# An attention and gMLP block on one core: weight differences behind the softmax scaling, and rotation tables by one transpose

## The chip, the cores and the metric

The kernel runs on one core of a Trainium2 chip. The metric is the device time in microseconds. A core has a matrix engine (TensorE, PE in the profile), VectorE (DVE), ScalarE (ACT), GpSimd (POOL) and SyncE (SP), which here only issues transfers. ACT and POOL issue transfers too, in the same queue of instructions as their other work. Each engine takes its own queue in order, and an instruction waits for semaphores that other engines and transfers raise.

## The reference

One block over 1024 positions of width 1024, all in float32: an RMS norm, one input projection, windowed attention with sinks, a gated branch with position mixing, two merge gates, an output projection, the residual and a last RMS norm. What matters here is the attention's part:

```python
q = partial_rope(q.reshape(B, S, ATT_HEADS, HEAD_DIM), pos)
k = partial_rope(k.reshape(B, S, ATT_KV_HEADS, HEAD_DIM), pos)
...
m = jnp.maximum(jnp.max(s, axis=-1, keepdims=True), sink)
p = jnp.exp(s - m)
denom = jnp.sum(p, axis=-1, keepdims=True) + jnp.exp(sink - m)
o = jnp.einsum('bhgnqk,bnkhd->bnqhgd', p / denom, vb.astype(jnp.float32))
```

There are 16 query heads of 64 and 2 heads of keys and values; the window goes by chunks of 64 positions. `partial_rope` turns the first 16 of the 64 values of a head by the cosine and sine of a position times 8 frequencies, so the tables hold 8 x 1024 numbers each.

## The kernel before, in words

**Products.** Every projection goes by a scheme of seven products in place of eight (Strassen's). `gemm_pair` makes one pair of row blocks: seven times `product`, 12 matmuls each of 128x512, in the order b11, t1, t2, b21, t3, b22, t4. Each operand is split in two float32r parts, a high one (`wh`) and a low one (`wl`), and a product is made of high times high, high times low and low times high. The weights of the next pair are split while the present one runs: four times per pair `split_next` takes the next halves (`wr` loaded, or `s`, the sums that the scheme needs) and calls `split`: ACT casts the high part (L176) and DVE subtracts it, which leaves the low part (L177, the *weight difference*). With 1024 columns it serves two products.

**Stages in order.** First norms and the gMLP's parts; then one pair for keys and values; then four pairs for q (m = 0, 2, 4, 6), during which keys and q are rotated; then eleven pairs for the gates z, gs and ga, into whose hooks the attention's steps are woven; then the gated branches, the merge and the output projection.

**The attention's steps.** There are 32. For each chunk `softmax_stage` has two score matmuls (L1445), copies on ACT (L1451), one bound per half on DVE (L1457: sum of two halves and their row minimum), and the exponential on ACT (L1473). At the step's end it takes the sink's exponential (L1487, L1488), adds it to the sums (L1489), takes the reciprocal (L1491) and scales the weights `pr` with it (L1497). `weight_stage` turns the scaled weights by PE transposes (L1518); `value_stage` multiplies them with the values (L1553, L1558).

**Order.** The code of pairs and steps is interleaved by hooks between the products. A scheduler then orders each engine's queue by its own estimates of when things are ready, and `after(a, b)` adds an order between two instructions of one engine without a wait.

**Tables.** In the q stage the rotation (by DVE, on rows that are turned so that positions lie along the row) needs the tables as 128x512 tiles: row (half, head, frequency), column position. `rope_tables`, a generator that runs in the hooks of the second q pair (m = 2), loads cos and sin with positions on the partitions, spreads them on DVE (L1221, eight copies), turns them on PE (L1228, eight transposes in two groups of four) and copies each table out on ACT (L1229). The steps of `steps_of_q` run one after the other: tables first, then the keys' rotations, then q's.

**Transfers.** The stores of q and the loads of weights go through SP's queue, the stores of keys and values through POOL's, and ACT's queue has no transfer but a load at the start (L109). Eight semaphores go round among the transfers that SP and ACT issue: each waits until the one that used its semaphore before is done.

Of the kernel before, what the change touches and what calls it, by code (L numbers as in the profile page):

```python
# [24 lines left out]
F32 = mybir.dt.float32  # L25
# [5 lines left out]
P = 128  # L31
D = 1024
S = 1024
KC = D // P
HALF = 512
NT = S // P
# [16 lines left out]
def hybrid_tile(  # L53
# [16 lines left out]
    nc = tc.nc  # L70
# [42 lines left out]
    ident = const.tile([P, P], F32, name="ident")  # L113
# [21 lines left out]
    k_dr = scratch("k_dr", (P, 4, S))  # L135
    v_dr = scratch("v_dr", (NT, P, 2, 3 * HD))
    s1_dr = scratch("s1_dr")
    z_dr = scratch("z_dr")
    gs_dr = scratch("gs_dr")
    ga_dr = scratch("ga_dr")  # L140
# [26 lines left out]
    hi_of, lo_of = [], []  # L167
# [51 lines left out]

    of_units = []  # L220
    bounds = []
    sums_behind = []

    def split_next():

        if not units:
            begin_job()
        if not units:
            return
        halves, keys = units.pop(0)  # L230
        if keys[0][1] == 2:
            make_sums(term_of_x11[0] if done[0] <= 4 else None)
        hi = mtile([P, D], F32R, "wh", 3)
        lo = mtile([P, D], F32R, "wl", 3)
        if isinstance(halves, list):
            for c, half in enumerate(halves):
                split(hi[:, half_of(c)], lo[:, half_of(c)], half)
        else:
            wide = halves.shape[1]
            first = split(hi[:, 0:wide], lo[:, 0:wide], halves)  # L240
            if keys[0] == (done[0] - 1, 6) and done[0] > LAST_OF_Q + 2:
                if bounds:
                    sums_behind.append(first)
                else:
                    make_sums(first)
        of_units.append(hi_of[-1])
        for c, key in enumerate(keys):
            ready[key] = hi[:, half_of(c)], lo[:, half_of(c)]
        if len(units) == 1:
            begin_job()  # L250

    def half_of(half):
        return slice(half * HALF, (half + 1) * HALF)
# [19 lines left out]
    def make_sums(first=None):  # L273

        while sums_to_make:
            sums_to_make.pop(0)(first)
# [269 lines left out]
    pool = outer.enter_context(tc.tile_pool(name="mixing", bufs=1))  # L546
# [527 lines left out]
    late = []  # L1074
# [82 lines left out]
    pool = stage.enter_context(tc.tile_pool(name="keys", bufs=1))  # L1157
# [32 lines left out]
    def finish(i, half, q, src, sign):  # L1190
        if sign < 0:
            nc.scalar.mul(q[:], src, sign)
        (values_of if i else keys_of)(half, q)

    gemm_pair(hb, finish, hook)
    stage.close()

# [4 lines left out]
    pool = stage.enter_context(tc.tile_pool(name="queries", bufs=1))  # L1202
    split_pool = stage.enter_context(tc.tile_pool(name="split", bufs=1))
    SC = -(HD**-0.5)
    tables = []

    def rot_tile():
        return mtile([P, HALF], F32, "rot", 5, pool)

    both = rot_tile()[:, 0 : 2 * NT * 16].rearrange("p (f t d) -> p f t d", f=2, t=NT)  # L1210

    def rope_tables():

        for f, src in enumerate((cos, sin)):
            nc.sync.dma_start(both[:, f], src)
        yield
        for src in (both[:, 0, :, 0:8], both[:, 1, :, 8:16]):
            tab = mtile([P, HALF], F32, f"tab{len(tables)}", 1, pool)
            wide = rot_tile()
            for i in range(4):  # L1220
                nc.vector.tensor_copy(  # L1221
                    wide[:, i * P : (i + 1) * P].rearrange("p (a h d) -> p a h d", a=2, h=8),
                    src[:, i : i + 5 : 4, :].unsqueeze(2).broadcast_to([P, 2, 8, 8]),
                )
            yield
            pt = bank("tp")
            for i in range(4):
                nc.tensor.transpose(pt[:, i * P : (i + 1) * P], wide[:, i * P : (i + 1) * P], ident[:])  # L1228
            nc.scalar.copy(tab[:], pt[:])  # L1229
            tables.append(tab)  # L1230
            yield

# [103 lines left out]
    for m in range(0, KC, 2):  # L1336

        def finish(i, half, q, src, sign):
            if sign < 0:
                nc.scalar.mul(q[:], src, sign)  # L1340
            put(q_raw, m + i, half, q[:])
            rows = slice((m + i) * P, (m + i + 1) * P)
            split_q(q[:], [(slice(0, P), q_hl[:, rows, half_of(half)].rearrange("a p t -> p a t"))])

        if m == 2:
            steps_of_q.append(rope_tables())
        if m == 4:
            steps_of_q.append(rotate_keys(0))
            steps_of_q.append(rotate(0, 3))
        gemm_pair(hb, finish, part_of_q)  # L1350
# [76 lines left out]
    def softmax_stage(g, t, par, qt):  # L1427

        kt = keys[g, t][0]
        q_of = qt[:].rearrange("p i (q c) -> p c (i q)", c=2)
        nmax, sums = small(), small()
        n_pr[0] += 1
        pr = mtile([P, 2, 384], F32, f"pr{n_pr[0] % 2}", 1, weights_pool)
        held_in = {}
        sinks_of = (v[:, 4 * g + par : 4 * g + par + 3 : 2] for v in (sink_sb, nsink_sb))
        sk, nsk = sinks_of
        for c in range(2):
            lo, hi = window_of(t, c)  # L1440
            wide = hi - lo
            scores, halves, copies = [], [], []
            for i in range(2):
                sc = bank("sc")[:, 0 : 2 * wide].rearrange("p (f k) -> p f k", f=2)
                nc.tensor.matmul(  # L1445
                    sc, q_of[:, c, i * P : (i + 1) * P], kt[:, :, lo:hi], start=True, stop=True
                )
                scores.append(sc)
            for i, sc in enumerate(scores):
                two = mtile([P, 2, 192], F32, "sl", 2, aheads)[:, :, 0:wide]  # L1450
                copies.append(nc.scalar.copy(two, sc))  # L1451
                halves.append(two)
            for i, two in enumerate(halves):
                at = 192 * (1 - c) if t else P * (1 - c)
                held_in[c, i] = v = pr[:, i, at : at + wide]
                bounds.append(
                    nc.vector.tensor_tensor_reduce(  # L1457
                        v,
                        two[:, 0, :],
                        two[:, 1, :],  # L1460
                        1.0,
                        nsk[:, i : i + 1],
                        op0=ALU.add,
                        op1=ALU.min,
                        accum_out=nmax[:, 1 - c, i : i + 1],
                    )
                )
# [12 lines left out]

            unfinished.append(rest_of_chunk)
            if c == 0:
                yield

        def rest_of_step():
            es = small()
            nc.vector.tensor_add(es[:], sk.unsqueeze(1).broadcast_to([P, 2, 2]), nmax[:])  # L1487
            nc.scalar.activation(es[:], es[:], AF.Exp)  # L1488
            nc.vector.tensor_add(es[:], es[:], sums[:])  # L1489
            inv = small()  # L1490
            nc.vector.reciprocal(inv[:], es[:])  # L1491
            spans = ((0, 2, 384),) if t else ((0, 1, P), (1, 1, 64))
            start = 0
            for first, chunks, wide in spans:
                v = pr[:, :, start : start + wide].rearrange("p i (c k) -> p i c k", c=chunks)
                by = inv[:, first : first + chunks].rearrange("p c i -> p i c").unsqueeze(3)
                nc.vector.tensor_mul(v, v, by.broadcast_to(list(v.shape)))  # L1497
                start += wide
            held.append(pr)

        yield
# [531 lines left out]
    for p in range(4):  # L2033
# [93 lines left out]
        wide = HALF // 2  # L2127
# [98 lines left out]
```

## Time and profile before

| what | us |
|---|---|
| median of 3 runs | 890.01 (889.78 to 890.14) |
| the profiled execution, its time | 890.97 |
| the profiled execution, its span | 889.2 |
| DVE COPY of the tables (L1221), x8 | 0.22 each |
| ACT COPY of the tables (L1229), x2 | 0.59 each |
| PE transposes of the tables (L1228), from 232.1 to 238.4 | 8 |
| attention's transposes (L1518), from 315.8 to 573.2 | 184 |

The page gives busy times of each engine over the span. A row of a timeline has the start, the duration, the engine, the line, the operation, and out<-in by the program's names; behind it in brackets stands how long the engine had been idle and what released it. A row of the chain of waits has the start, the length, the engine, what it made and the line: it is the work that ended last, followed back from the end, step by step to what released it. A matmul's duration overlaps that of the next, so what a matmul costs is read from the distance of two starts.

### The profile page before, as it was taken

What the parts mean: (1) busy time and instruction counts of PE and PEld (TensorE: products, weight loads), DVE (VectorE), ACT (ScalarE), POOL (GpSimd) and SP (SyncE); (2) the same over time, 40 slices, a digit from 0 to 9 for tenths busy, and PEclk for the clock granted to TensorE, in tenths of its full rate; (3) what the DMA queues carried; (4) which work ended last, traced back from release to release, by engine and by line L of the source; (5) the groups of instructions that cost most, each with busy time, mean ns of one, the idle gap of its engine ahead of it and who ended that gap; (6) DMA issues with size and microseconds to landing.
All of it is one profiled execution on the core that took longest, in us unless ns stands there. A gap on an engine that the chain in (4) does not pass through costs nothing.

```text
span 889.2 us, 13055 instructions
## 1 busy us (share of the span) xinstructions
PE 879.4 (99%) x4117; PEld 731.3 (82%) x4117; DVE 696.5 (78%) x1334; ACT 557.0 (63%) x1125; POOL 150.9 (17%) x217
## 2 busy tenths in 40 slices
PE   9999999999999999999999999999999999999996
PEld 6888888888888888888888888888888888888885
DVE  7869966566687679989888999847796587579886
ACT  6865533334455478888878888864684485467443
POOL 3322222203030001111211111101121121110012
PEclk9999999999999999999999999999999999999999
DMA  9998888958778666887786789989899789998533
GB/s 331 217 266 220 269 206 177 172 153 259 257 256 282 215 198 182 217 187 191 179 242 227 227 234 232 240 303 375 310 294 373 270 233 253 299 308 285 177 120 118
DMA packets 131409, 212.39 MB, mean 239 GB/s; under 512 B 12778, under 2 KB 59882, under 8 KB 131340
## 3 DMA queue, kind: packets, MB, share of 16 engines
q1 hardware_dynamic: 108808, 148.62, 49.9%
q0 software_dynamic: 22384, 62.67, 31.6%
q8 instruction: 33, 0.54, 0.2%
q14 instruction: 36, 0.29, 0.1%
q10 hardware_dynamic: 148, 0.27, 0.1%
HBM read 146.37 MB, written 86.11 MB: 261 GB/s over the span
## 4 chain that ended last, share of the span: by engine, by line
PE 93%; DMA 2%; DVE 2%; ACT 2%; issue 1%; SPq 0%; ACTq 0%
PE ps_mm L362 44%; PE ps_o L362 23%; PE ps_tp L362 7%; PE ps_sc L362 3%; PE ps_tp L796 2%; PE ps_sc L1445 2%; PE ps_tp L1518 2%; PE ps_o L796 2%; PE ps_mm L796 2%; PE ps_tp L1115 2%; PE ps_o L1553 1%; PE ps_sc L796 1%; DMA T_t1l<-in_x_dram 1%; DMA T_t3h<-in_w_dram 1%; PE ps_o L1558 1%
## 5 line engine op out<-in xcount | busy, mean ns | idle before, releaser
L176 ACT CAST wh<-s 128x1024 fp32r<-128x1024 f32 (+1 forms) x79 | 79.4, 1007 | 75.2 <-PE ps_mm L362 23.2
L177 DVE TENSOR_TENSOR wl<-wr,wh 128x512 fp32r<-128x512 f32 (+1 forms) x77 | 72.0, 936 | 59.9 <-ACT wh L176 56.5
L176 ACT CAST wh<-wr 128x512 fp32r<-128x512 f32 (+1 forms) x77 | 63.1, 820 | 61.1 <-PE ps_mm L362 38.7
L177 DVE TENSOR_TENSOR wl<-s,wh 128x1024 fp32r<-128x1024 f32 (+1 forms) x79 | 92.8, 1175 | 10.2 <-ACT wh L176 10.1
L1451 ACT COPY sl<-ps_sc 128x384 f32<-128x384 f32 (+2 forms) x128 | 52.0, 458 | 15.5 <-DVE sm L1457 11.5
L362 PE MATMUL ps_o<-T_t1h,wh 128*128 128x512 f32 x148 | 58.0, 392 | 0.0
L362 PE MATMUL ps_o<-T_t1h,wl 128*128 128x512 f32 x148 | 57.8, 390 | 0.0
L362 PE MATMUL ps_o<-T_t1l,wh 128*128 128x512 f32 x148 | 57.6, 389 | 0.0
L1473 ACT ACTIVATE pr<-pr,sm 128x192 f32<-128x192 f32 (+2 forms) x128 | 56.6, 450 | 0.0
L362 PE MATMUL ps_mm<-T_b11h,wh 128*128 128x512 f32 x140 | 54.9, 392 | 0.0
L362 PE MATMUL ps_mm<-T_b11l,wh 128*128 128x512 f32 x140 | 54.6, 390 | 0.0
L362 PE MATMUL ps_mm<-T_t3h,wh 128*128 128x512 f32 x140 | 54.6, 390 | 0.0
L362 PE MATMUL ps_mm<-T_t2l,wh 128*128 128x512 f32 x140 | 54.6, 390 | 0.0
L362 PE MATMUL ps_mm<-T_t2h,wh 128*128 128x512 f32 x140 | 54.6, 390 | 0.0
L362 PE MATMUL ps_mm<-T_t3l,wh 128*128 128x512 f32 x140 | 54.6, 390 | 0.0
L362 PE MATMUL ps_mm<-T_b11h,wl 128*128 128x512 f32 x140 | 54.6, 390 | 0.0
L362 PE MATMUL ps_mm<-T_t3h,wl 128*128 128x512 f32 x140 | 54.6, 390 | 0.0
L362 PE MATMUL ps_mm<-T_t2h,wl 128*128 128x512 f32 x140 | 54.5, 389 | 0.0
L362 PE MATMUL ps_mm<-T_t4h,wh 128*128 128x512 f32 x136 | 53.2, 391 | 0.0
L362 PE MATMUL ps_mm<-T_t4h,wl 128*128 128x512 f32 x136 | 53.0, 390 | 0.0
L362 PE MATMUL ps_mm<-T_t4l,wh 128*128 128x512 f32 x136 | 52.9, 389 | 0.0
L1457 DVE CUSTOM_DVE_ANT_0 pr<-sl,nsink_sb 128x192 f32<-128x192 f32 (+2 forms) x128 | 47.3, 400 | 3.5 <-ACT sl L1451 2.5
(431 smaller groups left out, 2435.3 us busy)
## 6 DMA issues: line engine op xcount, KB each, us to landing
wr<-in_w_dram SPq DMA_DIRECT2D x86, 256.0 KB
sums<-in_w_dram POOLq DMA_DIRECT2D x20, 512.0 KB, 6.8
s<-sums SPq DMA_DIRECT2D x20, 512.0 KB
q_hl<-qhl SPq DMA_DIRECT2D x16, 512.0 KB
q<-q_hl SPq DMA_DIRECT2D x64, 128.0 KB
y_dr<-x POOLq DMA_DIRECT2D x28, 256.0 KB, 6.9
g<-in_w_dram POOLq DMA_DIRECT2D x12, 512.0 KB, 6.8
wr<-in_w_dram SPq DMA_DIRECT2D x11, 512.0 KB
```

Of the source, the lines that this page charges most:

```text
L176: hi_of.append(nc.scalar.copy(hi, src))
L177: lo_of.append(nc.vector.tensor_sub(lo, src, hi.bitcast(F32)))
L362: nc.tensor.matmul(acc, lt, rt, start=fresh and k == 0 and n == 0, stop=k == 3 and n == 2, skip_group_check=True,)
L796: mm = nc.tensor.matmul(acc[:], lt, rt, start=fresh and k == 0 and n == 0, stop=stops and k == 3 and n == terms[-1], skip_group_check=True,)
L1115: nc.tensor.matmul(pm[:, t * P : (t + 1) * P], xh[:, half * 4 + t, g * P : (g + 1) * P], bias[-1][1][:, g % 4, :], start=True, stop=True,)
L1445: nc.tensor.matmul(sc, q_of[:, c, i * P : (i + 1) * P], kt[:, :, lo:hi], start=True, stop=True)
L1451: copies.append(nc.scalar.copy(two, sc))
L1457: nc.vector.tensor_tensor_reduce(v, two[:, 0, :], two[:, 1, :], 1.0, nsk[:, i : i + 1], op0=ALU.add, op1=ALU.min, accum_out=nmax[:, 1 - c, ...
L1473: e = nc.scalar.activation(v, v, AF.Exp, bias=nmax[:, 1 - c, i : i + 1], scale=-1.0, accum_out=sums[:, 1 - c, i : i + 1])
L1518: nc.tensor.transpose(dst, pr[:, i, block * P : block * P + width], ident[:])
L1553: nc.tensor.matmul(po[:, first], va[1][:, vs], a[:, n, first], start=n == 0, stop=n == 1, skip_group_check=True)
L1558: nc.tensor.matmul(po[:, cs], vb[c][:, vs], b[c][:], start=t == 0, stop=True, skip_group_check=True)
```

## The change

It has two parts.

**The differences.** The list `scaled_steps` collects the scalings. Once there are bounds and a scaling, `split_next` puts each weight difference that it issues behind the last scaling that has been issued, on DVE, by `after`.

**The tables.** In the pair for keys and values, cos and sin are loaded on SP (`load_tables`) into a tile of their own, two DVE copies put the 8 used columns of each beside one another (`pack_tables`, 128x64 each), one PE transpose of 128x128 turns both, ACT copies the result (`turn_tables`), and two transfers on ACT's queue store it to a scratch tensor `rope_dr` in DRAM. In the q stage `rope_tables` loads each table from there by two transfers on ACT's queue, which read every row eight times, once for each head. The generator joins `steps_of_q` at the first q pair (m = 0) in place of the second, so what follows it, the rotation of the keys, can begin earlier.

```diff
     def split_next():
...
+        if bounds and scaled_steps:
+            after(lo_of[-1], scaled_steps[-1])
         of_units.append(hi_of[-1])
...
+    def load_tables():
+        for f, src in enumerate((cos, sin)):
+            nc.sync.dma_start(both[:, f], src)
+
+    def pack_tables():
+        for f in range(2):
+            nc.vector.tensor_copy(
+                narrow[:, 64 * f : 64 * f + 64].rearrange("p (n d) -> p n d", n=NT),
+                both[:, f, :, 8 * f : 8 * f + 8],
+            )
+
+    def turn_tables():
+        pt = bank("tp")
+        nc.tensor.transpose(pt[:, 0:P], narrow[:], ident[:])
+        nc.scalar.copy(turned[:], pt[:, 0:P])
+        for f in range(2):
+            nc.scalar.dma_start(rope_dr[f].rearrange("d (n p) -> n d p", n=NT), turned[64 * f : 64 * f + 64])
...
+    late += [load_tables, pause, pause, pause, pack_tables, pause, pause, turn_tables]
     gemm_pair(hb, finish, hook)
...
     def rope_tables():
-        for f, src in enumerate((cos, sin)):
-            nc.sync.dma_start(both[:, f], src)
-        yield
-        for src in (both[:, 0, :, 0:8], both[:, 1, :, 8:16]):
-            tab = mtile([P, HALF], F32, f"tab{len(tables)}", 1, pool)
-            wide = rot_tile()
-            for i in range(4):
-                nc.vector.tensor_copy(
-                    wide[:, i * P : (i + 1) * P].rearrange("p (a h d) -> p a h d", a=2, h=8),
-                    src[:, i : i + 5 : 4, :].unsqueeze(2).broadcast_to([P, 2, 8, 8]),
-                )
-            yield
-            pt = bank("tp")
-            for i in range(4):
-                nc.tensor.transpose(pt[:, i * P : (i + 1) * P], wide[:, i * P : (i + 1) * P], ident[:])
-            nc.scalar.copy(tab[:], pt[:])
+        for f in range(2):
+            tab = mtile([P, HALF], F32, f"tab{f}", 1, pool)
+            for half in range(2):
+                nc.scalar.dma_start(
+                    tab[64 * half : 64 * half + 64],
+                    rope_dr[f][:, half_of(half)].unsqueeze(0).broadcast_to([8, 8, HALF]),
+                )
             tables.append(tab)
             yield
...
-        if m == 2:
+        if m == 0:
             steps_of_q.append(rope_tables())
...
-                nc.vector.tensor_mul(v, v, by.broadcast_to(list(v.shape)))
+                scaled_steps.append(nc.vector.tensor_mul(v, v, by.broadcast_to(list(v.shape))))
```

How this moves instructions. The lines of the changed kernel are higher by 1 up to the list, by 4 up to the tables and by 18 behind them.

DVE before, at the end of a step in the second gate pair (around 348 us of the span); `sm` are sums and bounds, `ISA` is a bound, `pr` the softmax weights:

```order
L1487 TENSOR_TENSOR sm_3287<-sink_sb,sm_3166 128x4
L404 TENSOR_TENSOR x_3045<-x_3045,ps_o_3095 128x512
L1489 TENSOR_TENSOR sm_3287<-sm_3287,sm_3167 128x4
L177 TENSOR_TENSOR wl_3309<-s_3019,wh_3308 128x1024
L1491 RECIPROCAL sm_3291<-sm_3287 128x4
L1457 ISA pr_557_3274,sm_3272<-sl_3316,nsink_sb 128x192
L1457 ISA sm_3272 128x1
L1497 TENSOR_TENSOR pr_531_3168<-pr_531_3168,sm_3291 128x768
L1457 ISA pr_557_3274,sm_3272<-sl_3318,nsink_sb 128x192
L1457 ISA sm_3272 128x1
L177 TENSOR_TENSOR wl_3343<-s_3020,wh_3342 128x1024
```

The same place of DVE after the change:

```order
L1505 TENSOR_TENSOR sm_3279<-sink_sb,sm_3158 128x4
L408 TENSOR_TENSOR x_3037<-x_3037,ps_o_3087 128x512
L1507 TENSOR_TENSOR sm_3279<-sm_3279,sm_3159 128x4
L1475 ISA pr_556_3266,sm_3264<-sl_3308,nsink_sb 128x192
L1475 ISA sm_3264 128x1
L1509 RECIPROCAL sm_3283<-sm_3279 128x4
L1475 ISA pr_556_3266,sm_3264<-sl_3310,nsink_sb 128x192
L1475 ISA sm_3264 128x1
L1515 TENSOR_TENSOR pr_530_3160<-pr_530_3160,sm_3283 128x768
L178 TENSOR_TENSOR wl_3301<-s_3011,wh_3300 128x1024
L178 TENSOR_TENSOR wl_3335<-s_3012,wh_3334 128x1024
```

The first difference has moved from ahead of the reciprocal to behind the scaling, and the second bound has moved ahead of the scaling. It is so in nine pairs; at step 1 the difference moves behind the scaling too, and there PE's four transposes go ahead of two score matmuls that they followed. On ACT the two exponentials that need these bounds go ahead of an eviction (L535) that they followed.

PE before, in the second q pair, where the first of the two groups of table transposes stands between products t2 and b21:

```order
L362 MATMUL ps_mm_2059<-T_t2h_693,wh_2019 128x512
L362 MATMUL ps_mm_2059<-T_t2l_694,wh_2019 128x512
L362 MATMUL ps_mm_2059<-T_t2h_693,wl_2020 128x512
L1228 MATMUL ps_tp_2115<-ident,rot_2093 128x128 x4
L362 MATMUL ps_o_2121<-T_b21h_142,wh_1973 128x512
L362 MATMUL ps_o_2121<-T_b21l_143,wh_1973 128x512
```

PE after, in the pair for keys and values, between products b21 and t3:

```order
L366 MATMUL ps_o_1782<-T_b21h_143,wh_1615 128x512
L366 MATMUL ps_o_1782<-T_b21l_144,wh_1615 128x512
L366 MATMUL ps_o_1782<-T_b21h_143,wl_1616 128x512
L1215 MATMUL ps_tp_1809<-ident,narrow_1728 128x128
L366 MATMUL ps_mm_1730<-T_t3h_755,wh_1688 128x512
L366 MATMUL ps_mm_1730<-T_t3l_756,wh_1688 128x512
```

Both groups of four are gone from the second q pair, and one transpose has come into the pair before the q stage.

ACT before, in the first q pair (from about 213 us on); `qhl` is a q cast, `x` an eviction:

```order
L176 CAST wh_1973<-wr_1872 128x1024
L1240 ACTIVATE qhl_1968<-x_1906 128x4x2x64
L1240 ACTIVATE qhl_1991<-x_1908 128x4x2x64
L176 CAST wh_2019<-s_1882 128x1024
L1240 ACTIVATE qhl_2010<-x_1907 128x4x2x64
L176 CAST wh_2043<-s_1883 128x1024
L1340 ACTIVATE x_2035<-ps_mm_1905 128x512
```

ACT after, at the same place:

```order
L177 CAST wh_1991<-wr_1885 128x1024
L1258 ACTIVATE qhl_1986<-x_1918 128x4x2x64
L1244 DMA tab_298_1934<-rope_dr 64x1x512 x2
L1244 DMA tab_300_1951<-rope_dr 64x1x512 x2
L1258 ACTIVATE qhl_2009<-x_1920 128x4x2x64
L1258 ACTIVATE qhl_2028<-x_1919 128x4x2x64
L177 CAST wh_2037<-s_1895 128x1024
L177 CAST wh_2061<-s_1896 128x1024
L1358 ACTIVATE x_2053<-ps_mm_1917 128x512
```

The four table loads stand behind the first q cast, and one more q cast now stands ahead of the cast of the weights for product t1 of the next pair. POOL's order is unchanged. On SP, the two loads of cos and sin stand among the sums' stores of the pair for keys and values, and the loads for the rotation of the keys come earlier by part of a pair.

More of the change, by code (lines that the diff above doesn't have):

```diff
@@ L137, in hybrid_tile @@
     s1_dr = scratch("s1_dr")
+    rope_dr = scratch("rope_dr", (2, 8, S))
     z_dr = scratch("z_dr")
@@ L221, in hybrid_tile @@
     bounds = []
+    scaled_steps = []
     sums_behind = []
@@ L1193, in finish, with pause @@
         (values_of if i else keys_of)(half, q)
+    both = mtile([P, 2, NT, 16], F32, "both", 1, pool)
+    narrow, turned = (mtile([P, P], F32, tag, 1, pool) for tag in ("narrow", "turned"))
+    def load_tables():
[13 more added lines that the diff above has]
+            nc.scalar.dma_start(rope_dr[f].rearrange("d (n p) -> n d p", n=NT), turned[64 * f : 64 * f + 64])
+    def pause():
+        pass
+    late += [load_tables, pause, pause, pause, pack_tables, pause, pause, turn_tables]
     gemm_pair(hb, finish, hook)
@@ L1208, in rot_tile @@
         return mtile([P, HALF], F32, "rot", 5, pool)
-    both = rot_tile()[:, 0 : 2 * NT * 16].rearrange("p (f t d) -> p f t d", f=2, t=NT)
     def rope_tables():
-        for f, src in enumerate((cos, sin)):
-            nc.sync.dma_start(both[:, f], src)
-        yield
-        for src in (both[:, 0, :, 0:8], both[:, 1, :, 8:16]):
-            tab = mtile([P, HALF], F32, f"tab{len(tables)}", 1, pool)
-            wide = rot_tile()
-            for i in range(4):
-                nc.vector.tensor_copy(
-                    wide[:, i * P : (i + 1) * P].rearrange("p (a h d) -> p a h d", a=2, h=8),
-                    src[:, i : i + 5 : 4, :].unsqueeze(2).broadcast_to([P, 2, 8, 8]),
-                )
-            yield
-            pt = bank("tp")
-            for i in range(4):
-                nc.tensor.transpose(pt[:, i * P : (i + 1) * P], wide[:, i * P : (i + 1) * P], ident[:])
-            nc.scalar.copy(tab[:], pt[:])
+        for f in range(2):
[4 more added lines that the diff above has]
+                    rope_dr[f][:, half_of(half)].unsqueeze(0).broadcast_to([8, 8, HALF]),
+                )
             tables.append(tab)
```

## The prediction

> **What bounds the kernel now.** I read the page's busy table and its chain first, then what PE waits for, then the chain and the timelines at single places.
>
> ```profile
> span 889.2 us, 13055 instructions
> PE 879.4 (99%) x4117; PEld 731.3 (82%) x4117; DVE 696.5 (78%) x1334; ACT 557.0 (63%) x1125; POOL 150.9 (17%) x217
> PE 93%; DMA 2%; DVE 2%; ACT 2%; issue 1%; SPq 0%; ACTq 0%
> PE ps_tp L1518 <- DVE pr L1497: 0.6, 2, 0.4
> ```
>
> PE is busy for 99% of the span and carries 93% of the chain. So only two things are worth time: work taken off PE, and moments in which PE stands still. Work taken off DVE (78%) or ACT (63%) is worth nothing by itself. The fourth line is the only wait of PE inside the attention stage that the waits name: the transposes of the softmax weights (L1518) stood for the scaling on DVE (L1497), twice, 0.6 us in all. Since matmul ends are modelled, I don't trust that sum and go by starts instead: matmuls of one product start 0.22 or 0.23 us apart.
>
> ```profile
> 349.68 0.39 PE L362 MATMUL ps_mm<-T_b11h,wl 128*128 128x512 f32 x1
> 350.46 0.30 PE L1518 MATMUL ps_tp<-ident,pr 128*128 128x128 f32 x1 [0.40 <-DVE pr L1497]
> 375.67 0.39 PE L362 MATMUL ps_mm<-T_b11h,wl 128*128 128x512 f32 x1
> 375.90 0.27 PE L1518 MATMUL ps_tp<-ident,pr 128*128 128x128 f32 x1
> 401.07 0.39 PE L362 MATMUL ps_mm<-T_b11h,wl 128*128 128x512 f32 x1
> 401.53 0.30 PE L1518 MATMUL ps_tp<-ident,pr 128*128 128x128 f32 x1
> 501.48 0.39 PE L362 MATMUL ps_mm<-T_b11h,wl 128*128 128x512 f32 x1
> 501.89 0.30 PE L1518 MATMUL ps_tp<-ident,pr 128*128 128x128 f32 x1
> 552.50 0.39 PE L362 MATMUL ps_mm<-T_b11h,wl 128*128 128x512 f32 x1
> 552.96 0.30 PE L1518 MATMUL ps_tp<-ident,pr 128*128 128x128 f32 x1
> ```
>
> At 375.67 the transposes follow after 0.23, with no stall. At 349.68 they follow after 0.78, at 401.07 after 0.46, at 501.48 after 0.41 and at 552.50 after 0.46. The stalls are 0.55, 0.23, 0.18 and 0.23: **1.19 us**, twice what the waits name. All stand at the same point, between the first product of a pair (b11) and the transposes of a step.
>
> **The change, part 1: the weight difference behind the scaling.** What DVE does just ahead of the largest stall:
>
> ```profile
> 347.74 0.16 DVE L1489 TENSOR_TENSOR sm<-sm,sm 128x4 f32<-128x4 f32 x1
> 347.82 1.22 DVE L177 TENSOR_TENSOR wl<-s,wh 128x1024 fp32r<-128x1024 f32 x1
> 348.96 0.17 DVE L1491 RECIPROCAL sm<-sm 128x4 f32<-128x4 f32 x1
> 349.05 0.39 DVE L1457 CUSTOM_DVE_ANT_0 pr<-sl,nsink_sb 128x192 f32<-128x192 f32 x1
> 349.36 0.95 DVE L1497 TENSOR_TENSOR pr<-pr,sm 128x768 f32<-128x768 f32 x1
> 350.23 0.41 DVE L1457 CUSTOM_DVE_ANT_0 pr<-sl,nsink_sb 128x192 f32<-128x192 f32 x1
> 350.57 1.22 DVE L177 TENSOR_TENSOR wl<-s,wh 128x1024 fp32r<-128x1024 f32 x1
> ```
>
> A difference of 1.22 us stands between the sums and their reciprocal. Starts give the slots: the difference 1.14 (347.82 to 348.96), the reciprocal 0.09, a bound 0.31 to 0.34, the scaling 0.87. The new order has sums, bound, reciprocal, bound, scaling, difference, difference. So the scaling loses 1.14 ahead of it and gains one bound (0.34): it starts at 349.36 - 1.14 + 0.34 = 348.56 and ends at 349.51. PE started 0.15 after the scaling's end (350.31 to 350.46), so it could start at 349.66. The end of the product allows 349.68 + 0.23 = 349.91. The stall is gone with 0.25 us to spare; at the other three places it was smaller by 0.3 or more for the same move, so these go too. I take all of 1.19; the bounds are 0 (something else is late there) and 1.19.
>
> What is late next? The first difference now runs from 349.43 to 350.65 and the second ends where it did. The first one's reader is the third matmul of the pair's second product:
>
> ```profile
> 351.97 0.40 PE L362 MATMUL ps_o<-T_t1h,wl 128*128 128x512 f32 x1
> 325.69 0.61 PE ps_tp L1518 x4
> 350.46 0.85 PE ps_tp L1518 x6
> ```
>
> Without the stall it stands at 351.97 - 0.55 = 351.42, and with 0.15 for the hand-over the difference has to end by 351.27: 0.62 us of slack. At step 1 (325.69) the four transposes only change places with two score matmuls; I take nothing there.
>
> **Part 2: one transpose for eight.**
>
> ```profile
> 229.57 2.72 PE ps_mm L362 x12
> 232.30 0.50 PE ps_tp L1228 x4
> 232.79 2.76 PE ps_o L362 x12
> 238.28 0.44 PE ps_tp L1228 x4
> L1221 DVE COPY rot<-rot x8: 218/219/220, 231.8 to 232.7; 128x128 f32<-128x128 f32 x8
> L1229 ACT COPY tab<-ps_tp x2: 587/590/592, 233.1 to 238.8; 128x512 f32<-128x512 f32 x2
> ```
>
> The eight old transposes stand on PE's chain with 0.50 + 0.44 = 0.94 us, between products with no gap, so all of it goes. The product behind one costs 2.76 for 2.72, which I leave inside the error. One transpose comes instead, between two products of the key and value pair. No row shows a lone one. From the rows above, four cost 0.61 and six 0.85 in the softmax, so 0.12 each and 0.61 - 3 x 0.12 = 0.25 for one; from 0.44 it is 0.44 - 3 x 0.12 = 0.08. I take 0.20, nearer to the row with the same matmuls on both sides of a step; the bounds are 0.08 and 0.25. The net is **0.74 us** (0.69 to 0.86). The Trainium skill, "TensorE: Matmul & The Clock Gate", section "Part 4: PE-mode transpose", gives about 275 ns for one 128x128 transpose inside a kernel (in bf16); by that price, an estimate, the net would be 0.66 and the sum 0.08 less. This trace doesn't show a lone one in fp32.
>
> The 8 copies on DVE (8 x 0.219 = 1.8 us) and the 2 on ACT (1.2 us) are worth nothing, since PE didn't wait for either engine there; nor do the two new copies of 128x64 and one of 128x128 cost anything, as long as they arrive before PE's new transpose some 10 us later.
>
> **Part 3: six DMAs on ACT's queue.** The two stores of the turned table stand where ACT idled before, and two loads more on SP stand ahead of stores of the sums. The four table loads stand in ACT's queue right behind the first q cast of the first q pair:
>
> ```profile
> 216.74 0.67 ACT L1240 ACTIVATE qhl<-x 128x512 fp32r<-128x512 f32 x1
> 219.45 0.66 ACT L1240 ACTIVATE qhl<-x 128x512 fp32r<-128x512 f32 x1 [2.04 <-DVE x L398]
> 221.28 1.05 ACT L176 CAST wh<-s 128x1024 fp32r<-128x1024 f32 x1 [1.17 <-PE ps_o L362]
> 214.44 2.53 SPq L212 DMA_DIRECT2D wr<-in_w_dram  x4
> 217.07 0.54 SPq L523 DMA_DIRECT2D q_raw<-x  x1
> 212.39 0.77 POOL L1183 DMA_DIRECT2D v_dr<-vt  x1 [3.70 <-issue]
> 216.59 0.53 POOL L1258 MEMSET rot<- 128x512 f32 x1 [3.43 <-DMA v_dr<-vt]
> 227.14 0.39 PE L362 MATMUL ps_o<-T_t1h,wl 128*128 128x512 f32 x1
> y_dr<-x POOLq DMA_DIRECT2D x28, 256.0 KB, 6.9
> ```
>
> Their waits are: the last store of the values (landed by 216.59), the stores of the table, and, since eight semaphores go round among the DMAs of SP and ACT, the weight loads of 214.44 and the q store of 217.07. Behind them in ACT's queue stand two q casts (0.66 each) and the cast of the weights for the next pair's second product (1.05), behind which DVE makes the difference (1.22) that PE reads at 227.14. Counted back: 227.14 - 0.15 - 1.22 - 1.05 - 0.66 - 0.66 = 223.4 is when ACT must be free at the latest. Without any wait it is free at 217.41 + 4 x 0.54 = 219.57 (0.54 is the issue of a store above). How long a store of 256 KB takes to land on SP's queue no row shows; the value store of 212.39 needed 4.2 us, which gives 217.07 + 4.2 + 0.54 = 221.8: 1.6 us of slack. I take no cost; the bounds are 0 and 1.1 (if it lands after 6.9 us, the median of POOL's stores y_dr on the page: 217.07 + 6.9 + 0.54 = 224.5).
>
> The Trainium skill, "DMA: Bandwidth & Descriptors", section "Anatomy of one DMA — SWDGE (gpsimd) path", says that DMA engines never wait on semaphores and that the issuing engine's sequencer does it before dispatch. This rule speaks against putting such loads on a computing engine; it is the mechanism of the third case below, and no run so far shows it, as ACT's queue carries one load only (L109) before the change.
>
> POOL's own order doesn't move. On SP the loads for the key rotation come earlier, and PE waits for nothing of theirs.
>
> **Sum.** 1.19 + 0.74 = 1.93 us. The profiled execution took 890.97 (span 889.2 and 1.8 around it), 0.96 above the median of 890.01. 890.97 - 1.93 = 889.04 for a profiled one, and 890.01 - 1.93 = **888.1** for the median. A measurement of this kernel can tell about 0.2% from no change, which is 1.78 us, so the forecast lies just beyond that bound.
>
> **The rivals.**
>
> 1. *The scaling isn't what PE waited for alone.* If ACT's work for the same step, or the second bound in front, keeps the transposes late, only the tables and a part of the stalls remain: 0.74 + 0.3 = 1.0, 889.0. For it speaks that the spare time at 349.9 is only 0.25 us; against it, that the scaling's end and PE's start lie 0.15 apart at every stall.
> 2. *The second bound becomes the late one (slower).* The scaling now stands behind both bounds, and these wait for ACT's copies of the scores. If the copy for the second one comes late by d, the four stalling pairs lose d - 0.25 each, on top of a gain of 1.93. The point is 4 x (d - 0.25) = 1.93, d = 0.73 us; with d = 1.2 the loss is 3.8 - 1.9 = 1.9 us: 891.9. The row below is ACT's two copies of that step: they are done at 346.75 + 0.86 = 347.61, and the second bound now starts at about 348.25, 0.64 later, which speaks against it; for it speaks only that ACT's order moves around there.
>
> ```profile
> 346.75 0.86 ACT L1451 COPY sl<-ps_sc 128x384 f32<-128x384 f32 x2 [2.35 <-DVE sm L1457]
> ```
>
> 3. *ACT stands at the table loads.* At 6.9 us of landing PE loses 224.5 - 223.4 = 1.1 us once, and the result is 889.2; at 8 us it is 890.3. A pair later ACT has caught up, because it is busy for only 63%.
> 4. *More goes than counted*: the 0.04 behind a transpose, the changed places at step 1, another short stall. 887.7.
>
> **How the numbers follow.** The forecast has 0.55, and with 0.3 us either way about four fifths of it lie beyond 0.2%: 0.44 faster, 0.11 same. Rival 1 has 0.17 and rival 3 0.12, both same; rival 2 has 0.10, slower; rival 4 has 0.06, faster. Faster 0.50, same 0.40, slower 0.10. The range goes from 887.5, below rival 4, to 889.8, above rivals 1 and 3 up to a landing of 7.5 us; rival 2 and the tail of 3 are left out.
>
> **What the profile of after would show.** Right: the waits of PE name L1515 (the scaling's new line) once at most, at the last step near 571 us, which isn't reordered; b11's last matmul and the transposes lie 0.23 apart in every pair; no wait of PE for a weight difference; the rows of L1228 are gone from the chain and one transpose stands at about 197 us. Wrong: gaps above 0.23 at those places (rival 1 or 2; the releaser of the second bound tells which), a wait of PE for the weights between 226 and 230 us, or ACT idle there until after 223.4 (rival 3).

## The result, and the profile after

| | median us | range | runs |
|---|---|---|---|
| before | 890.2 | 889.78 to 890.79 | 9 |
| after | 887.84 | 887.17 to 889.1 | 9 |

The ratio is 0.9971, with a 95% interval of 0.9963 to 0.998: faster by 2.4 us of the medians, and by 1.8 to 3.3 us by the interval. The profiled execution of `diffs_only` was disturbed (3160 us) and is left out of its median, so that part's trace is read from `diffs_only_2`.

The page after the change: the busy times, and the chain by engine.

```profile
span 885.7 us, 13043 instructions
PE 877.2 (99%) x4110; PEld 731.4 (83%) x4110; DVE 696.2 (79%) x1328; ACT 555.3 (63%) x1124; POOL 151.6 (17%) x217
PE 97%; ACT 1%; DVE 1%; issue 0%; DMA 0%; ACTq 0%
```

What PE waits for after the change (in all, times, longest), the one line inside the attention stage:

```profile
PE ps_tp L1536 <- DVE pr L1515: 0.2, 1, 0.2
```

DVE and ACT are as busy as before. PE's share of the chain has gone from 93% to 97%, as the chain leaves PE less often. Of the two waits for the scaling one is left, at the last step; it stood there before too (0.17 of the 0.6 us). PE's timeline after the change, at the four places that had a stall:

```profile
348.00 0.39 PE L366 MATMUL ps_mm<-T_b11h,wl 128*128 128x512 f32 x1
348.23 0.81 PE L1536 MATMUL ps_tp<-ident,pr 128*128 128x128 f32 x6
398.80 0.39 PE L366 MATMUL ps_mm<-T_b11h,wl 128*128 128x512 f32 x1
399.03 0.27 PE L1536 MATMUL ps_tp<-ident,pr 128*128 128x128 f32 x1
498.94 0.39 PE L366 MATMUL ps_mm<-T_b11h,wl 128*128 128x512 f32 x1
499.17 0.27 PE L1536 MATMUL ps_tp<-ident,pr 128*128 128x128 f32 x1
549.74 0.39 PE L366 MATMUL ps_mm<-T_b11h,wl 128*128 128x512 f32 x1
549.97 0.27 PE L1536 MATMUL ps_tp<-ident,pr 128*128 128x128 f32 x1
```

Each distance is 0.23 us; they were 0.78, 0.46, 0.41 and 0.46. All 1.19 us are gone, and a little more goes with them, because the matmuls behind a stall run a little slower. From b11's last matmul to the third matmul of the next product, with the transposes and two scores between, it was 351.97 - 349.68 = 2.29 us at the first place and is 349.70 - 348.00 = 1.70: 0.59 less, where the distance alone says 0.55. At the other three the same stretch is shorter by 0.27, 0.23 and 0.28. That is 1.37 us in all.

Six transposes in the chain of waits, before the change at a place without a stall (the prediction shows 0.85 for the six at 350.46, behind a stall):

```profile
376.06 0.65 PE ps_tp L1518 x6
```

And after the change at the first of the four places:

```profile
348.39 0.65 PE ps_tp L1536 x6
```

The chain counts a row behind a stall from its own start, and other rows from the end of the matmul before, so 0.85 and 0.65 don't compare as prices. By starts the six cost 0.60 behind the stall (350.46 to 351.06, where the scores start) and 0.57 after the change (348.23 to 348.80).

The timeline of DVE at the first of these places, and in the last line PE's reader of the first difference:

```profile
346.03 0.16 DVE L1507 TENSOR_TENSOR sm<-sm,sm 128x4 f32<-128x4 f32 x1
346.11 0.41 DVE L1475 CUSTOM_DVE_ANT_0 pr<-sl,nsink_sb 128x192 f32<-128x192 f32 x1
346.86 0.95 DVE L1515 TENSOR_TENSOR pr<-pr,sm 128x768 f32<-128x768 f32 x1
347.73 2.35 DVE L178 TENSOR_TENSOR wl<-s,wh 128x1024 fp32r<-128x1024 f32 x2
349.70 0.40 PE L366 MATMUL ps_o<-T_t1h,wl 128*128 128x512 f32 x1
```

The scaling begins 0.83 us behind the start of the sums (it was 1.62), and ends at 347.81, 0.42 before PE takes it. The first of the two differences ends at about 348.9, 0.8 us before its reader at 349.70.

The tables, in the chain of waits (start, length, what):

```profile
192.51 2.72 PE ps_o L366 x12
195.23 0.11 PE ps_tp L1215
195.34 2.75 PE ps_mm L366 x12
```

The one new transpose costs 0.11 us, and the product behind it 2.75 for 2.72. The two groups of four (0.50 and 0.44) are gone from the second q pair. The rotation of the keys hardly begins earlier: its first multiplication starts at 240.6 us, 58.3 behind the last group of the position mixing (182.35), where it was 59.2 behind (242.1 and 182.92). The difference is about what PE has gained by then. The chain at step 1 after the change:

```profile
323.88 0.44 PE ps_tp L1536 x4
324.32 0.35 PE ps_sc L1463 x2
```

And the row of the chain before, which stood ahead of the four transposes at 325.69:

```profile
325.34 0.35 PE ps_sc L1445 x2
```

Together these six matmuls cost 0.79 us; with the scores first they cost 0.35 + 0.61 = 0.96. By starts, from b11's last matmul to the third of the next product, it was 1.67 us and is 1.47. So a short stall stood here too: the transposes started 0.50 behind two scores that cost 0.35. And ACT's queue in the first q pair, after the change (ACTq is an issue), with PE's reader of the difference made from that cast:

```profile
216.27 0.67 ACT L1258 ACTIVATE qhl<-x 128x512 fp32r<-128x512 f32 x1
216.64 3.22 ACTq L1244 DMA_DIRECT2D tab<-rope_dr  x4
219.91 0.66 ACT L1258 ACTIVATE qhl<-x 128x512 fp32r<-128x512 f32 x1 [2.97 <-DMA tab<-rope_dr]
221.70 0.67 ACT L1258 ACTIVATE qhl<-x 128x512 fp32r<-128x512 f32 x1 [1.13 <-DVE x L408]
222.26 1.03 ACT L177 CAST wh<-s 128x1024 fp32r<-128x1024 f32 x1
226.67 0.39 PE L366 MATMUL ps_o<-T_t1h,wl 128*128 128x512 f32 x1
```

The four loads hold ACT for 3.22 us, and ACT is free at 219.9. Taken one by one, they start at 216.64, 217.31, 217.98 and 219.28: the first three are 0.67 apart, and the fourth comes 0.63 later than that spacing. The last two:

```profile
217.98 0.58 ACTq L1244 DMA_DIRECT2D tab<-rope_dr  x1
219.28 0.58 ACTq L1244 DMA_DIRECT2D tab<-rope_dr  x1
```

No row names what the fourth waited for. The latest moment at which ACT had to be free, worked out in the prediction, was 223.4, 222.9 in this execution, which is 0.5 us earlier at this place.

### The profile page after: what moved, and what is told of

It is laid out like the page before. It is cut to its first block, busy times and chain, and to the rows that moved or that the text cites. A ratio compares the mean times of both kernels' runs of the same rounds, so it can differ in the third digit from the quotient of the medians.

```text
span 885.7 us, 13043 instructions
## 1 busy us (share of the span) xinstructions
PE 877.2 (99%) x4110; PEld 731.4 (83%) x4110; DVE 696.2 (79%) x1328; ACT 555.3 (63%) x1124; POOL 151.6 (17%) x217
## 4 chain that ended last, share of the span: by engine, by line
PE 97%; ACT 1%; DVE 1%; issue 0%; DMA 0%; ACTq 0%
PE ps_mm L366 46%; PE ps_o L366 24%; PE ps_tp L366 7%; PE ps_sc L366 3%; PE ps_o L800 3%; PE ps_mm L800 2%; PE ps_tp L800 2%; PE ps_sc L1463 2%; PE ps_tp L1536 2%; PE ps_tp L1119 2%; PE ps_o L1571 1%; PE ps_sc L800 1%; PE ps_sc L670 1%; PE ps_o L1576 1%; DMA wr<-in_x_dram 0%
```

## The experiments

All times are medians; before is 890.2 to 890.8 us in the same calls. To tell parts of a tenth of a microsecond apart I read landmarks on PE and not the whole time: from the last group of the gMLP's position mixing (around 182 us) to the first softmax transpose for the tables, and from there to the start of the last step's transposes for the attention. Each landmark is read in one execution, the profiled one.

| kernel | median us | ratio to before (95%) | mixing to first transpose, us | first to last step's, us |
|---|---|---|---|---|
| before | 890.2 | | 132.91 | 256.79 |
| after | 887.84 | 0.9971 (0.9963 to 0.998) | 132.02 | 255.17 |
| diffs_only / diffs_only_2 | 889.11 / 889.32 | 0.9982 (0.9973 to 0.9991) / 0.9985 (0.9976 to 0.9995) | 132.84 (diffs_only_2) | 255.34 (diffs_only_2) |
| tables_only | 889.39 | 0.9985 (0.9977 to 0.9994) | 132.10 | 256.73 |
| stalling_pairs_only | 888.13 | 0.9973 (0.9962 to 0.9984) | 132.21 | 255.39 |
| other_pairs_only | 889.0 | 0.9978 (0.9969 to 0.9987) | 131.96 | 257.24 |
| tabs_on_sp | 887.68 | 0.9964 (0.9949 to 0.9978) | 131.99 | 255.16 |
| tabs_later | 887.98 | 0.9965 (0.9952 to 0.9978) | 132.09 | 255.15 |
| last_scaling_first | 887.9 | 0.9977 (0.9968 to 0.9986) | 132.01 | 254.78 |
| last_scaling_and_lows | 887.97 | 0.997 (0.9959 to 0.9981) | 131.96 | 254.78 |
| diff_twice | 895.82 | 1.0054 (1.0039 to 1.0069) | 131.99 | 262.75 |

**The two parts alone.** `diffs_only` is the kernel before with the first part of the diff, `tables_only` the changed kernel without these lines:

```diff
-        if bounds and scaled_steps:
-            after(lo_of[-1], scaled_steps[-1])
```

> The kernel before with the first part alone: weight differences behind the scaling, tables as before. Theory (the stalls in front of L1518 are what it removes): 1.19 us from the four stalls plus 0.24 us at step 1, 1.4 us faster than before (about 888.8 beside 890.2); every b11 to L1518 distance 0.23. Rival (the tables carry the gain and the stalls come back elsewhere): within 0.3 us of before.

> The changed kernel without the order between difference and scaling: the tables' part alone. Theory (PE time of seven transposes in two groups): 0.8 to 0.9 us faster than before (about 889.3), the stalls of 0.55, 0.23, 0.18 and 0.23 us stand at the same places as before. Rival (an earlier rotation or the loads on ACT's queue move more than that): over 1.5 us faster, or no gain.

> The first part alone once more, for a profile of it. Theory: the time of the run before (889.2) within 0.5 us; no gap in front of L1518 but the last one near 571 us; the eight table transposes of L1228 stand on PE's chain with 0.94 us as in the kernel before. Rival (tables and differences share a gain): a gap of 0.2 us or more at one of the four places, or a table group that costs less than 0.4 us.

The differences alone give 1.6 and 1.1 us in two calls, the tables alone 1.3 (0.5 to 2.0); by the landmarks the differences take 256.79 - 255.34 = 1.45 us off the attention and nothing off the tables' stretch, and the tables take 0.81 off theirs and nothing off the attention. PE's timeline without the new order (`tables_only`):

```profile
349.76 0.39 PE L364 MATMUL ps_mm<-T_b11h,wl 128*128 128x512 f32 x1
350.50 0.30 PE L1534 MATMUL ps_tp<-ident,pr 128*128 128x128 f32 x1 [0.36 <-DVE pr L1513]
```

PE's timeline with it alone (`diffs_only_2`):

```profile
348.95 0.39 PE L365 MATMUL ps_mm<-T_b11h,wl 128*128 128x512 f32 x1
349.18 0.60 PE L1521 MATMUL ps_tp<-ident,pr 128*128 128x128 f32 x4
```

The tables' groups on the chain of `diffs_only_2`:

```profile
231.86 0.44 PE ps_tp L1231 x4
237.77 0.44 PE ps_tp L1231 x4
```

The stall stands in the one (0.74 between starts) and is gone in the other (0.23), where the table groups still cost 0.88. Without the new order all four stalls are there, 0.51, 0.24, 0.18 and 0.24; with it alone none is. The two parts alone add up to 1.45 + 0.81 = 2.26 us by the landmarks, both together give 1.62 + 0.89 = 2.51. The difference is no more than such stretches differ between executions of the same work, so nothing shows that the parts need each other. The expected 889.3 for the tables and 888.8 for the differences were met within 0.6 us.

**Where in the attention the gain sits.** Two kernels keep the order in half of the pairs each (`done` counts pairs; the other kernel has 1 for 0):

```diff
-        if bounds and scaled_steps:
+        if bounds and scaled_steps and done[0] % 2 == 0:
```

> The changed kernel with the order kept only in every second gate pair, the ones around 350, 401, 452, 501 and 552 us, four of which had a stall; step 1 and the pairs between keep the old order. Theory (the gain sits at those stalls): 0.24 us slower than the changed kernel, all of it at step 1 near 325 us. Rival (the new order helps in each pair by a little): half of 1.4 us is lost, 0.7 us slower.

> The mirror of the run before: the order is kept at step 1 and in the pairs around 375, 426, 476 and 527 us, which had no stall, and the old order stands around 350, 401, 452, 501 and 552 us. Theory (the gain sits at the stalls): the four stalls of 0.55, 0.23, 0.18 and 0.23 us are back, 1.2 us slower than the changed kernel (about 889.0). Rival (each pair gains a little): 0.7 us slower.

With the order in the stalling pairs only, the median is 888.13, 0.3 us above the changed kernel, and the one gap that is back is step 1's, where 0.50 lie between the scores and the transposes. With the order in the other pairs only, it is 889.0, 1.2 us above. These medians come from other calls than the changed kernel's, with medians of before that were about 0.5 us higher, so the landmarks decide: the first loses 255.39 - 255.17 = 0.22 us, the second 257.24 - 255.17 = 2.07. PE's timeline of the first at step 1:

```profile
323.70 0.51 PE L1463 MATMUL ps_sc<-k,q 128*128 128x384 f32 x2
324.20 0.52 PE L1536 MATMUL ps_tp<-ident,pr 128*128 128x128 f32 x3
```

PE's timeline of the second:

```profile
347.91 0.39 PE L366 MATMUL ps_mm<-T_b11h,wl 128*128 128x512 f32 x1
348.65 0.41 PE L1536 MATMUL ps_tp<-ident,pr 128*128 128x128 f32 x2 [0.35 <-DVE pr L1515]
```

The four gaps of the second are 0.51, 0.25, 0.19 and 0.25 above the 0.23 of a product. The reorder gains nothing where nothing waited, and the rival of a little in each pair (0.7 us for both) falls. The second kernel loses more than the stalls: of its 2.07 us the four gaps make 1.20, or about 1.35 with the slower matmuls behind them. About 0.7 lie at one more place, where two scores at 552.50 wait for ACT's cast (0.5 us among the waits); neither the kernel before nor the changed one has this wait. Why that comes there was not tried, so the hit of the median on the expected 889.0 is partly chance.

**Doubling the cost.** The tables' part alone, with the difference made twice ahead of the scaling in nine pairs:

```diff
+        if bounds and 5 < len(scaled_steps) < 34 and keys[0][1] == 2:
+            wide = halves.shape[1]
+            again = nc.vector.tensor_sub(lo[:, 0:wide], halves, hi[:, 0:wide].bitcast(F32))
+            after(scaled_steps[-1], again)
```

> The kernel with the tables' part alone, and in nine pairs the difference ahead of the scaling is made twice (the same result written again), so that 1.14 us more of DVE stand ahead of the scaling. In some pairs the two score matmuls (0.45 us) now go ahead of the transposes and cover that much. Theory (PE waits for the scaling, one for one): distances from b11 or the scores to L1518 grow by 0.4 to 1.14 us in each of the nine pairs, 4 to 8 us slower than the tables' part alone (893 to 897). Rival (the scaling isn't what PE waits for): under 2 us slower.

895.82, 6.4 us above `tables_only`. What PE waits for in it:

```profile
PE ps_tp L1538 <- DVE pr L1517: 3.8, 11, 0.7
```

PE's timeline at the first of the nine places:

```profile
349.42 0.39 PE L368 MATMUL ps_o<-T_t1l,wh 128*128 128x512 f32 x1
350.50 0.85 PE L1538 MATMUL ps_tp<-ident,pr 128*128 128x128 f32 x6 [0.69 <-DVE pr L1517]
```

Two scores and two matmuls of the next product now stand ahead of the transposes, and still there is a gap of 1.08 - 0.23 = 0.85. At this place the account is even: the gap, two scores (0.35) and two matmuls (0.46) make 1.66 us, and the 0.51 of `tables_only` with 1.14 more are 1.65. At the three other places that had stalled, the gap and the scores make 1.08 to 1.09, where 1.32 to 1.38 were due. In eight of the nine pairs gaps of 0.28 to 0.85 stand there, 4.4 us in all; the ninth, near 452 us, where the scaling comes in two short parts (128x256 and 128x128), has none. The expectation did not name a second place: in the same eight pairs another 0.21 to 0.46 stand ahead of the next step's transposes, most of them behind product t2, 2.3 us in all. The trace puts those that it names there down to the scaling too. So PE waits for the scaling, which is the expectation's mechanism; one for one holds at the first place only.

**The table loads.** `tabs_on_sp` issues the four loads on SP, `tabs_later` joins the generator at m == 2 again:

```diff
-                nc.scalar.dma_start(
+                nc.sync.dma_start(
```

> The changed kernel with the four table loads on SP's queue in place of ACT's. Theory (ACT had 2.9 us to spare behind the loads): PE runs as in the changed kernel, within 0.3 us. Rival (ACT's wait of 3.2 us is paid in part): faster by more than 0.5 us; other rival (SP's weight loads behind the table loads come late): slower, with PE or DVE waiting for wr loads.

> The changed kernel with the table loads in the second q pair, as before the change, in place of the first. Theory (an earlier rotation of the keys is worth nothing, since PE waits for none of it): within 0.3 us of the changed kernel. Rival (the earlier start of the rotations is part of the gain): slower by 0.5 us or more, with stalls near the first scores at 300 to 325 us.

887.68 and 887.98, with 887.84 for the change: none of the three can be told from another, and their landmarks agree within 0.1 us. So ACT's hold costs nothing here. `tabs_later`, though, did not move what it was to move. Its table loads (count, durations, first and last start):

```profile
L1244 ACTq DMA_DIRECT2D tab<-rope_dr x4: 581/590/624, 217.1 to 222.5; - x4
```

They still stand in the first q pair, only spread among ACT's casts, and the keys' first multiplication starts at 241.0, 58.2 behind the last group of the mixing (182.76), as in the changed kernel. What an earlier rotation is worth was therefore not tried. The traces say only that it begins at most about 1 us earlier than before, and that no wait of PE for the rotation is named in either kernel.

**The stall that is left.** At the last step one more difference stands ahead of the scaling, because it is issued before there is that scaling to stand behind. `last_scaling_first` adds, where the last step has ended:

```diff
         finish_chunk()
+        after(lo_of[-1], scaled_steps[-1])
```

> The changed kernel with one more order: the last weight difference of the attention stage also stands behind the last scaling. Theory (the remaining 0.38 us before the last L1536 has the same cause): the distance there falls from 0.61 to 0.23 us, 0.3 to 0.4 us faster than the changed kernel (about 887.5), less up to 0.1 us for one matmul that now stands among these transposes. Rival (there it is the exponentials on ACT that are late): the distance stays above 0.5 us.

The scaling now ends about 2 us earlier, and the first four transposes wait no more (569.09 to 569.32). But the timeline shows a new gap two rows on, which the last row, DVE's, explains:

```profile
569.09 0.39 PE L366 MATMUL ps_o<-T_b22h,wl 128*128 128x512 f32 x1
569.32 0.63 PE L1536 MATMUL ps_tp<-ident,pr 128*128 128x128 f32 x4
569.71 0.47 PE L366 MATMUL ps_mm<-T_t4h,wh 128*128 128x512 f32 x1
570.27 0.41 PE L1536 MATMUL ps_tp<-ident,pr 128*128 128x128 f32 x2
569.27 0.85 DVE L1557 TENSOR_TENSOR pTb<-ps_tp,pTb 64x256 fp32r<-64x256 f32 x2
```

The two last transposes start at 570.27, 0.15 behind the end of the low parts that free their bank, the buffer that the transposes write (569.27 + 0.85 = 570.12): these stood behind the moved difference. The releaser isn't named in the row; the next run moves these low parts ahead, and this gap is gone. The stall had only passed on; the median of `last_scaling_first` is 887.9, no gain. The expectation named one misplaced matmul, but not this bank. So the difference was put behind the low parts too:

```diff
+        last_low = lo_of[-1]
...
             weigh(n)
+            if n == last - 2:
+                after(last_low, lows_of_pr[-1])
+                after(lows_of_pr[0], scaled_steps[-1])
```

> The changed kernel; at the last step DVE takes sums, reciprocal, scaling, the low parts of step 30's turned weights, and only then the weight difference, and PE's order is that of the changed kernel. Theory (in the run last_scaling_first the stall only passed from the scaling to the bank that these low parts free): the distance from b22's last matmul to L1536 is 0.23 us in place of 0.61, no slot of these transposes grows, 0.38 us faster than the changed kernel (about 887.5). Rival (something third is late, such as the exponentials on ACT): 0.2 us or more of the stall stays.

PE's timeline of it at the last step:

```profile
569.27 0.39 PE L366 MATMUL ps_o<-T_b22h,wl 128*128 128x512 f32 x1
569.50 0.81 PE L1537 MATMUL ps_tp<-ident,pr 128*128 128x128 f32 x6
```

No gap is left in front of a softmax transpose in the whole trace, and the stretch to the last step's transposes is 254.78 for 255.17, shorter by the stall. But this landmark stands ahead of the place to which the stall has now passed. The last value products of the attention, and in the last row DVE's low parts that they read:

```profile
574.10 0.39 PE L1577 MATMUL ps_o<-pTb,vb 128*128 128x256 f32 x1
574.64 0.36 PE L1577 MATMUL ps_o<-pTb,vb 128*128 128x256 f32 x1 [0.15 <-DVE pTb L1558]
573.62 0.88 DVE L1558 TENSOR_TENSOR pTb<-ps_tp,pTb 64x256 fp32r<-64x256 f32 x2
```

Two such products are 0.54 apart here, where two of them cost 0.23 or 0.24 in all at the other steps. From the first softmax transpose to the first matmul behind these products it takes 260.12 us, 260.00 in `last_scaling_first` and 260.00 in the changed kernel (261.64 before). So neither version gains anything: at the last step the time passed from the scaling to the bank, and from the bank to the value product. The expectation was right about the gap and wrong about the gain. The medians, 887.9 and 887.97 beside 887.84, agree.

## Why the prediction was right, point by point

The forecast was 1.93 us, from 890.01 to 888.1; measured were 2.4 us (1.8 to 3.3), to 887.84, inside the range of 887.5 to 889.8, and on the side that had the larger chance. The mechanism is shown; the sum was too small by about 0.5 us, as three of its terms erred the same way. The interval ends at 0.998, just at the 0.2% that the prediction named, and owes this to the terms that came out larger: 1.93 us lie only 0.15 beyond that bound. With 0.3 either way, spread evenly, three quarters of the forecast and not four fifths lie beyond it.

- **Four stalls, 1.19 us.** Right in place and cause: each distance is back to 0.23, and the two half kernels show that the gain sits there. The size was 1.37 us, as each stall also slowed the matmuls behind it by 0.04 or 0.05. Reading starts instead of the waits mattered more than the prediction says: of the 0.6 us that the waits named, 0.17 was the last step's, so only the largest of the four was named at all.
- **What is late next.** Right: nothing. The scaling's computed lead at 349.9 was 0.25 us, and the trace shows 0.42 - 0.15 = 0.27. The weight difference was to have 0.62 us of slack and has about 0.8 - 0.15 = 0.65.
- **Step 1, taken as nothing.** This term was mis-sized. The difference stood ahead of the scaling there too, so the transposes went behind the scores and still stood for a moment; 0.96 us on the chain became 0.79, 0.17 us (0.20 by starts), and the kernel that leaves out step 1 has its gap back.
- **One transpose for eight, 0.74 us.** Slightly small: the lone transpose costs 0.11 where I took 0.20 between 0.08 and 0.25, so 0.83, and the landmarks say 0.89 (132.91 to 132.02), 0.81 with the tables alone. The upper bound of 0.25 came from two rows that each stood behind a stall, 0.61 for four at step 1 and 0.85 for six at 350.46. Without a stall four have 0.44 and six 0.65 in the chain, so 0.11 each. The row between two products, which gave 0.08, was the nearer one. The price of 275 ns that the Trainium skill gives ("TensorE: Matmul & The Clock Gate", "Part 4: PE-mode transpose") is the duration in the row, 270 ns for it here, and not what it adds to PE's chain, 0.11.
- **ACT's hold.** Right that it costs nothing, with other numbers: the loads were 0.67 us apart, not 0.54, and the fourth came 0.63 later still; ACT was free at 219.9, well before the 221.8 that a wait for the q store was to give. Whether those 0.63 us are that wait, in a shorter form, stays open. The Trainium skill ("DMA: Bandwidth & Descriptors", "Anatomy of one DMA — SWDGE (gpsimd) path") says that a wait for a semaphore is served on the issuing sequencer before dispatch. The row fits this, as ACT's next cast stood 2.97 us for the loads, but no row here shows a semaphore wait by name.
- **The rivals.** A second late bound (slower) didn't come: the second bound began at 346.54, as soon as the reciprocal ahead of it left DVE, and the scaling followed at 346.86. That part of the stalls stays came true nowhere that the order changed; at the last step, where it didn't, 0.38 us stay, as the prediction had said of that place. What came nearest was the fourth rival, more than counted, which had the smallest chance and had named step 1.

The sum with the sizes that the runs showed is 1.37 + 0.20 + 0.83 = 2.4 us, and the landmarks give 1.62 + 0.89 = 2.5.

## What to carry to other kernels

On an engine with 99% busy time, read the distance of starts at the joints between its kinds of work, and compare with a joint that has none: a stall of 0.2 us doesn't appear among the waits, and four stalls, of which the waits named one, were half of this gain. Work that one engine makes ahead of its time (here weights for the next pair) belongs behind whatever the bounding engine takes next, as long as its own reader is further away than its length; and when a wait is taken away, look for the buffer or the reader that the moved work used to serve, since there the wait may only pass on. A gain of a few tenths is shown by landmarks inside the trace, with one part of the change in each kernel, not by medians. Put the last landmark behind the whole stage: one that stood at the old place of the stall showed 0.39 us of gain at the last step where there was none. And look in the trace whether an edit moved what it was to move; a new place in the code need not be a new place in the queue. Before the price of a group of instructions is read off a row, look whether the row stands behind a stall.

## What the runs showed of the hardware that was not expected

- Up to the last group of the position mixing all kernels of the table have the same instructions, yet this group starts at 181.93 us in one profile (`tabs_on_sp`) and at 183.77 in another (`tables_only`): 1.8 us of spread from the beginning of the kernel alone, most of the gain that was measured. Behind it, stretches with the same work agree within about 0.3 us.
- A lone transpose of 128x128 between products adds 0.11 us to PE's chain, a group of four 0.44 (0.50 once) and six 0.65, so about 0.11 each. Behind a stall the chain shows 0.61 for four and 0.85 for six, though by starts six cost only 0.03 more there.
- A stall costs PE a little more than the distance of starts says: 0.59 us for 0.55, and 0.27, 0.23 and 0.28 for 0.23, 0.18 and 0.23.
- In front of the softmax transposes the wait that the profile names is about 0.16 us shorter than the gap between starts: 0.40 for 0.55, 0.22 for 0.38, 0.69 for 0.85. That is what a matmul's row (0.39) is longer than the distance to the next (0.23).
- Four loads of 64x512 on ACT's queue hold it for 3.22 us; the first three start 0.67 apart, though one issue's row is 0.58 to 0.63 long.
